# Decoder trunk on one core: hop steps get priority, columns end where outputs or state are due, the embedding moves to other buffers

## Chip, cores and metric

The kernel runs on one core of a Trainium2 chip. The metric is the device time of one execution in microseconds, as the median of several runs.

## What is computed

One decoder layer on 512 tokens of width 2048, all in float32. Cut to what matters:

```python
h = rms_norm(x, norm_g)
z = h @ w_in                      # r,k,v,decay and rate inputs | rwkv gate | pool input | pool gate
zs = zs + (token_shift(zs) - zs) * mu
# RWKV group, 16 heads of 64:  S_t = S_{t-1}(diag(w_t) - kk_t^T (a_t kk_t)) + v_t^T k_t,  y_t = S_t r_t
y_rwkv = (head_group_norm(y) + bonus) * silu(g_rwkv)
# pool group, 4 groups of 256: window means over 2, 4, 8, 16 tokens minus the token
y_pool = (d @ w_pool) * pool_scale * silu(g_pool)
x = x + concat(y_rwkv, y_pool) @ w_out
x = x + sigmoid(x @ w_pg + b_pg) * (p @ w_ple)
return rms_norm(x, final_g)
```

The large products are made of three float32r products each (high x high, high x low, low x high). A weight tile is loaded by SyncE as `raw`, ScalarE converts it to `whi` (L132), VectorE takes the rest as `wlo` (L133). Activations are split the same way (L137, L138: `hhi`/`hlo`, `yhi`/`ylo`).

## The kernel before

Names: PE is TensorE, DVE is VectorE, ACT is ScalarE, SP is SyncE.

After the input norm the program runs eight rounds, one for each pair of heads (128 channels). A round's tokens are eight chunks of 64. The recurrence of a round goes from chunk to chunk by **hops**: `py<-sbd` (the state's part of the outputs, L753), `zs` on VectorE (L755), `pu<-zs` (L760), two copies `uv` on ScalarE (L763), `ps<-uv` (L768), and the state's two halves `sbd` on VectorE (L772 in the first chunk, L774 in others), which the next chunk's py reads. Each of these waits for the one before, so TensorE needs other work between them. That is the **stream**: the columns of `w_in` for the next round (`z` jobs), for the pool channels (`b` jobs, `pool_unit`), and at the end the embedding `p @ w_ple` (`embed_unit`). A column of 128 channels takes 48 products of 128x512 (`zcols`: 4 weight chunks of 12 products each). `pump(n)` takes products from the stream until n are done, and keeps a debt where it took more. `HC = (8, 8, 8)` says how many are wanted after each of the three products of a hop, and since they come in threes, links of six or nine arise. Halfway through a round `between()` pumps `H3` and `H2` products around `scores(j + 1)`, the next round's scores.

TensorE's instructions are kept in the order of the program (`pin`). VectorE, ScalarE and the queues get theirs from a scheduler, by priority and by its own estimate of when an operation is ready; each engine then runs its list in that order, so an operation that waits holds all behind it.

The pool (`pp`, two buffers a tag) holds the pool units' tiles `u`, `sw`, `sgp`, and `dh`/`dl` (one buffer each), the split input of the pool's product `wp`. The embedding's input `p` is transposed and split in the last round's `between()` into `hl`, which lies in the pool `rw` of the recurrence. Each embedding unit (512 columns) makes four row tiles `pple`; ScalarE copies each to `ple` (tags `u` and `sw`) and stores it to DRAM (L446, 256 KB).

After the rounds, the 16 tiles of the mixed output `yd` are loaded (`yin`, three buffers) and split to `yhi`/`ylo`, which lie where `rw` was: the first four by SP, the others by ACT (L891). Then comes the output projection (`acc_o`), weights `raw_o`/`whi_o`/`wlo_o`, and the gate product (`acc_g`). In the last 512 columns of it each of the four row tiles is finished in turn: `gate` adds the bias (L1012), takes tanh (L1013), and so on; `root` makes the norm's factor; `scaled` applies it and stores (L1053 for the last 512 columns, L1057 and L1059 for others).

Of the kernel before, what the change touches and what calls it, by code (L numbers as in the profile page):

```python
# [34 lines left out]
def trunk_kernel(ctx: ExitStack, tc: tile.TileContext, x, p, norm_g, w_in, mu, w0, w_up, a0, a_up,  # L35
# [157 lines left out]
    for j in range(NJ):  # L193
        if j + 1 < NJ:
            jobs += [("z", nm, j + 1) for nm in "krv"]
        jobs += [("b", None, n_ + i) for i in range(nfill[j])]
        n_ += nfill[j]
        if j + 1 < NJ:
            jobs += [("z", "g", j + 1)]
# [5 lines left out]
    for kind, nm, j in jobs:  # L205
        if kind == "z":
            plan_cols({"r": O_R, "k": O_K, "v": O_V, "g": O_G}[nm] + j * P, f"{nm}{j}")
        elif kind == "e":
# [174 lines left out]
    zt, dhl = {}, {}  # L383

    def zcols(ps, nm):
        for c in range(KT // CK):
            wh, wl = chunk(nm, c)
            for k in range(CK):
                kk = c * CK + k
                mm3(ps, wh[:, k, :], wl[:, k, :], hhi[:, kk, :], hlo[:, kk, :], kk == 0, kk == KT - 1)  # L390
                yield 3

    def pool_unit(n):
# [27 lines left out]
        for k in range(2):  # L421
            mm3(pq, wh[:, k, :], wl[:, k, :], dh[:, k, :], dl[:, k, :], k == 0, k == 1)
            yield 3
        m = 2 * g + i
        nc.vector.scalar_tensor_tensor(sgp, pq, dp(73, m), sgp, ALU.mult, ALU.mult)
        nc.scalar.dma_start(out=yd[NJ + m], in_=sgp)

    phl = []


    def embed_unit(ec):
        ws = [chunk(f"e{ec}_{k}", 0) for k in range(2)]
        phi, plo = phl
        for tt in range(NT):
            ts_ = slice(tt * P, (tt + 1) * P)
            pq = (psA, psM)[tt % 2].tile([P, EC], F32, name=f"pple{ec}_{tt}", tag=("acc", "m")[tt % 2])
            for k in range(2):
                wh, wl = ws[k]
                mm(pq, phi[:, k, ts_], wh[:, 0, :], start=k == 0, stop=False)
                mm(pq, phi[:, k, ts_], wl[:, 0, :], start=False, stop=False)  # L440
                mm(pq, plo[:, k, ts_], wh[:, 0, :], start=False, stop=k == 1)
                if k == 0:
                    yield 3
            t_ = pp.tile([P, EC], F32, name=f"ple{ec}_{tt}", tag=("u", "sw")[tt % 2])
            nc.scalar.copy(t_, pq)
            nc.scalar.dma_start(out=pled[ts_, ec * EC:(ec + 1) * EC], in_=t_)  # L446
            yield 3

    def stream():
        for kind, nm, j in jobs:  # L450
            if kind == "b":
                yield from pool_unit(j)
                continue
            if kind == "e":
                yield from embed_unit(j)
                continue
# [12 lines left out]
    def pump(n):  # L469
        debt[0] += n  # L470
        while debt[0] > 0:
            c = next(big, None)
            if c is None:
                debt[0] = 0
                return
            debt[0] -= c

    def need(nm, j):
# [246 lines left out]
    def recur(j, work, between):  # L725
# [17 lines left out]
        for ch in range(NCH):  # L743
# [8 lines left out]
            if ch > 0:  # L752
                mm(py[:, sl], ar[:, q, 2 * par:2 * par + 2, :], cur, start=ch in (1, 4), stop=True,  # L753
                                 skip_group_check=True)
                lead[0] = nc.vector.tensor_tensor(zs[pb:pb + 64], py[pb:pb + 64, sl], mv[pb:pb + 64, q, :], ALU.add)  # L755
                step()
# [4 lines left out]
            for h in range(2):  # L761
                hc = slice(64 * h, 64 * h + 64)
                nc.scalar.copy(uv[pb:pb + 64, ch, hc], psu[hc, hc])  # L763
            step()
            pump(HC2)
            if ch < NCH - 1:
                pss = psS.tile([P, T], F32, name=f"ps{j}_{ch}", tag="s")
                mm(pss[:, 0:P], bkn[:, ch, :], uv[:, ch, :], start=True, stop=True)  # L768
                for h in range(2):
                    hc = slice(64 * h, 64 * h + 64)  # L770
                    if ch == 0:
                        lead[0] = nc.vector.tensor_scalar(nxt[hc, hc], pss[hc, hc], pcc[hc], None, ALU.mult)  # L772
                    else:
                        lead[0] = nc.vector.scalar_tensor_tensor(nxt[hc, hc], pss[hc, hc], pcc[hc], s0p[hc, :],  # L774
                                                                 ALU.mult, ALU.add)
                s0p = rw.tile([P, C], F32, name=f"s0p{j}_{ch}", tag="s0p", bufs=2)
# [58 lines left out]
    HC, HT, HX = (8, 8, 8), 130, 16  # L835
    HS, HN = 9, 3
    pending = []
    need("k", 0)
# [13 lines left out]
    for j in range(NJ):  # L852
        def between():
            pump(H3)
            if j + 1 < NJ:
                scores(j + 1)
                pump(H2)
            else:

                phl.extend((hl[:, 0], hl[:, 1]))  # L860
                for k in range(2):
                    pt = psM.tile([P, T], F32, name=f"ppt{k}", tag="m")
                    for tt in range(NT):
                        tr(pt[:, tt * P:(tt + 1) * P], pn[:, tt, k * P:(k + 1) * P], ident)
                    split(phl[0][:, k, :], phl[1][:, k, :], pt)

        if j + 1 == NJ:
            pn = rw.tile([P, NT, DPLE], F32, name="pn", tag="ar", bufs=2)
            for h in range(2):
                nc.scalar.dma_start(out=pn[:, 2 * h:2 * h + 2, :],  # L870
                                    in_=p[256 * h:256 * h + 256, :].rearrange("(t p) q -> p t q", p=P))
            hl = rw.tile([P, 2, 2, T], F32R, name="hl", tag="mt", bufs=2)
        if j + 1 < NJ:
# [107 lines left out]
    with tc.tile_pool(name="fp", bufs=2) as fp, tc.tile_pool(name="kp_", bufs=1) as kp_:  # L981
# [20 lines left out]
        def gate(acc, ec, tt, cs, part):  # L1002
# [7 lines left out]
            else:  # L1010
                gt = fp.tile([P, w_], F32, name=f"gt{ec}_{tt}_{part}", tag="gt")
            nc.vector.tensor_tensor(gt, acc, bB[:, lc], ALU.add)  # L1012
            th = nc.scalar.activation(gt, gt, AF.Tanh, scale=0.5)  # L1013
# [12 lines left out]
            if ec < LAST:  # L1026
                nc.vector.tensor_tensor(x3[tt][:, cs], gt, gB[:, lc], ALU.mult)
            return gt, th, lead_

# [55 lines left out]
        for tt in range(NT):  # L1085
# [3 lines left out]
            for h, a_ in enumerate(acc[tt]):  # L1089
# [4 lines left out]
                with tc.high_priority(offset=TP * tt):  # L1094
                    g_, th_, lead_ = gate(a_, ec, tt, slice(ec * EC + hc.start, ec * EC + hc.stop), ec + h)
                gts.append(g_)
                if tt == NT - 1 and h == 1:
                    rs_, gts_ = rest
# [33 lines left out]
```

## Time and profile before

| | |
|---|---|
| median of 3 runs | 1124.58 us (1123.9 to 1125.92) |
| profiled execution | 1124.75 us |
| its span | 1123.0 us |
| mean granted TensorE clock | 0.991 of full speed |
| TensorE busy | 1080.0 us, 96% |
| VectorE / ScalarE / GpSimd busy | 63% / 40% / 6% |

TensorE is busy throughout, with three thin places: the start (input norm), the passage from the embedding to the output projection at some 743 to 752 us, and the end. The time between is 8 rounds of some 75 us from about 130 to 720, and two large projections from 752 to 1112. The view of waits names who ended each idle time of an engine; the timeline gives start, duration, engine, line and tiles of each instruction, and in brackets the idle time before it with its releaser. Matmuls are pipelined: one of 128x512 is shown with 0.39 us, but the next starts sooner.

### The profile page before, as it was taken

To read this page: it belongs to the slowest core of one execution; us is meant where nothing else is said; L and a number is where in the kernel's file an instruction comes from. 1 tells how busy PE (TensorE), PEld (TensorE's weight loads), DVE (VectorE), ACT (ScalarE), POOL (GpSimd) and SP (SyncE) were. 2 spreads that over 40 slices of the span, in tenths; PEclk is the share of its full clock that TensorE was granted. 3 is DMA by queue.
4 is the path that set the end of the run, shared out by engine and by line. 5 is a ranking of instruction groups with operands and counts; after the bars stand their busy time and mean duration, and the time that the engine had idled before them with its cause. 6 is when DMAs were issued, how large, how long until landed. Compare 5 with 4: busy or idle time off the path is not lost. (4 is left out here: it accounts for less than half of the span.)

```text
span 1123.0 us, 17267 instructions
## 1 busy us (share of the span) xinstructions
PE 1080.0 (96%) x6090; PEld 881.8 (79%) x6090; DVE 707.6 (63%) x1835; ACT 450.1 (40%) x917; POOL 68.5 (6%) x180
## 2 busy tenths in 40 slices
PE   5999999999999999999999999969999999999996
PEld 4888887877877877878778777758888888888885
DVE  7677868788579688786885946524424323345265
ACT  7633435334335353353352433444222222233246
POOL 2100110110010000201101001000000000000000
PEclk9999999999999999999999999979999999999998
DMA  7433432433423333323234332478434437355444
GB/s 228 121 92 93 109 97 76 110 87 80 114 80 100 102 83 91 97 76 108 81 91 118 90 117 66 136 252 256 163 99 164 136 127 227 111 188 144 146 132 150
DMA packets 178485, 138.56 MB, mean 123 GB/s; under 512 B 34677, under 2 KB 139742, under 8 KB 178398
## 3 DMA queue, kind: packets, MB, share of 16 engines
q1 hardware_dynamic: 158270, 104.94, 31.8%
q10 hardware_dynamic: 20128, 32.52, 9.1%
q8 instruction: 48, 0.79, 0.3%
q14 instruction: 39, 0.32, 0.1%
HBM read 118.02 MB, written 18.87 MB: 122 GB/s over the span
## 5 line engine op out<-in xcount | busy, mean ns | idle before, releaser
L133 DVE TENSOR_TENSOR wlo_g<-raw_g,whi_g 128x512 fp32r<-128x512 f32 x88 | 59.4, 684 | 85.7 <-ACT whi_g L132 83.4
L156 PE MATMUL acc_o<-whi_o,yhi 128*128 128x512 f32 x256 | 100.5, 396 | 9.3 <-ACT whi_o L132 9.3
L156 PE MATMUL zb<-hhi,whi_b 128*128 128x512 f32 x256 | 108.2, 423 | 0.0
L133 DVE TENSOR_TENSOR wlo_o<-raw_o,whi_o 128x512 fp32r<-128x512 f32 x64 | 43.9, 691 | 94.5 <-ACT whi_o L132 94.5
L132 ACT CAST whi_g<-raw_g 128x512 fp32r<-128x512 f32 x88 | 54.4, 621 | 118.0 <-PE acc_g L156 74.3
L156 PE MATMUL acc_o<-whi_o,ylo 128*128 128x512 f32 x256 | 101.3, 396 | 0.0
L156 PE MATMUL acc_o<-wlo_o,yhi 128*128 128x512 f32 x256 | 101.2, 395 | 0.0
L156 PE MATMUL zb<-hhi,wlo_b 128*128 128x512 f32 x256 | 100.7, 393 | 0.0
L156 PE MATMUL zb<-hlo,whi_b 128*128 128x512 f32 x256 | 100.0, 391 | 0.0
L156 PE MATMUL acc_g<-whi_g,x2hi 128*128 128x512 f32 (+1 forms) x224 | 86.8, 388 | 0.0
L156 PE MATMUL acc_g<-wlo_g,x2hi 128*128 128x512 f32 (+1 forms) x224 | 86.5, 386 | 0.0
L156 PE MATMUL acc_g<-whi_g,x2lo 128*128 128x512 f32 x224 | 86.1, 386 | 0.0
L132 ACT CAST whi_o<-raw_o 128x512 fp32r<-128x512 f32 x64 | 39.8, 623 | 100.5 <-PE acc_o L156 96.2
L132 ACT CAST whi_b<-raw_b 128x512 fp32r<-128x512 f32 x64 | 39.7, 620 | 76.2 <-PE zv L156 34.5
L781 POOL TENSOR_SCALAR s0p<-sbd,pw 64x64 f32<-64x64 f32 x96 | 48.8, 508 | 342.0 <-DVE sbd L774 257.1
L133 DVE TENSOR_TENSOR wlo_b<-raw_b,whi_b 128x512 fp32r<-128x512 f32 x64 | 43.9, 687 | 35.4 <-ACT whi_b L132 32.7
L156 PEld LDWEIGHTS acc_o<-whi_o,yhi 128*128 128x128 f32 x256 | 48.8, 191 | 19.6 <-issue 9.7
L156 PEld LDWEIGHTS acc_o<-wlo_o,yhi 128*128 128x128 f32 x256 | 48.8, 190 | 10.7 <-DVE wlo_o L133 0.5
L156 PEld LDWEIGHTS zb<-hhi,wlo_b 128*128 128x128 f32 x256 | 48.1, 188 | 11.2
L156 PEld LDWEIGHTS acc_o<-whi_o,ylo 128*128 128x128 f32 x256 | 48.8, 191 | 9.9
L630 DVE TENSOR_TENSOR xw<-xw,tm 128x60 f32<-128x60 f32 (+24 forms) x248 | 52.0, 210 | 6.7
L156 PEld LDWEIGHTS zb<-hhi,whi_b 128*128 128x128 f32 x256 | 48.4, 189 | 8.5
(281 smaller groups left out, 2537.9 us busy)
## 6 DMA issues: line engine op xcount, KB each, us to landing
raw_b<-in_w_in_dram SPq DMA_DIRECT2D x64, 256.0 KB
raw_o<-in_w_out_dram SPq DMA_DIRECT2D x64, 256.0 KB
raw_g<-in_w_pg_dram SPq DMA_DIRECT2D x64, 256.0 KB
raw_k<-in_w_in_dram SPq DMA_DIRECT2D x32, 256.0 KB
raw_r<-in_w_in_dram SPq DMA_DIRECT2D x32, 256.0 KB
raw_v<-in_w_in_dram SPq DMA_DIRECT2D x32, 256.0 KB
raw_g<-in_w_in_dram SPq DMA_DIRECT2D x32, 256.0 KB
n<-nd SPq DMA_DIRECT2D x16, 256.0 KB
```

The lines of the kernel that those rows point to most:

```text
L132: nc.scalar.copy(hi, raw)
L133: nc.vector.tensor_tensor(lo, raw, hi.bitcast(F32), ALU.subtract)
L156: i = nc.tensor.matmul(*a, **k)
L630: nc.vector.tensor_tensor(xw[:, 0:n_, s + 1:32], xw[:, 0:n_, s + 1:32], tm[:, 0:n_, 0:w_], ALU.add)
L781: nc.gpsimd.tensor_scalar(s0p[hc, :], nxt[hc, hc], pcn[hc], None, ALU.mult)
```

## The change

1. `zs`, `uv` and `sbd` are issued with a priority raised by `HP = 1000`, for the scheduler's order on VectorE and ScalarE.
2. The stream keeps its place within a column (`place`). After `scores(j + 1)` the new `pump_to(H2)` takes that many products that the place comes nearest to a multiple of 24 or to 6 beyond it. The pool units' six `wp` products are no longer counted. The last round's `between()` pumps 8 instead of `H3`.
3. The transposes and splits of `p` become a job of the stream ahead of pool unit 14. Their results lie in the tags `u` and `sw`, the embedding's row tiles in `dh`/`dl`, two row tiles a buffer: 8 stores of 512 KB instead of 16 of 256 KB. `hl` is gone.
4. In the tail, the scaling of the last 512 columns of tile tt - 1 is issued after the sum of tile tt (for tt 1 and 2).

```diff
@@ jobs
-        jobs += [("b", None, n_ + i) for i in range(nfill[j])]
+        for i in range(nfill[j]):
+            jobs += [("p", None, 0)] if n_ + i == 14 else []
+            jobs += [("b", None, n_ + i)]
@@ zcols
                 mm3(ps, wh[:, k, :], wl[:, k, :], hhi[:, kk, :], hlo[:, kk, :], kk == 0, kk == KT - 1)
+                place[0] = 3 * (kk + 1)
                 yield 3
@@ pool_unit
             mm3(pq, wh[:, k, :], wl[:, k, :], dh[:, k, :], dl[:, k, :], k == 0, k == 1)
-            yield 3
+            yield 0
@@ embed_unit
-        phi, plo = phl
+        outs = [pp.tile([P, 2, EC], F32, name=f"ple{ec}_{i}", tag=("dh", "dl")[i], bufs=1) for i in range(2)]
...
-            t_ = pp.tile([P, EC], F32, name=f"ple{ec}_{tt}", tag=("u", "sw")[tt % 2])
-            nc.scalar.copy(t_, pq)
-            nc.scalar.dma_start(out=pled[ts_, ec * EC:(ec + 1) * EC], in_=t_)
+            t_ = outs[tt // 2]
+            nc.scalar.copy(t_[:, tt % 2, :], pq)
+            if tt % 2 == 1:
+                rows = slice((tt - 1) * P, (tt + 1) * P)
+                nc.scalar.dma_start(out=pled[rows, ec * EC:(ec + 1) * EC].rearrange("(t p) n -> p t n", p=P), in_=t_)
@@ stream
+            if kind == "p":
+                for k in range(2):
+                    pt = psM.tile([P, T], F32, name=f"ppt{k}", tag="m")
+                    for tt in range(NT):
+                        tr(pt[:, tt * P:(tt + 1) * P], pn[0][:, tt, k * P:(k + 1) * P], ident)
+                    a_ = pp.tile([P, T], F32R, name=f"phi{k}", tag="u")
+                    b_ = pp.tile([P, T], F32R, name=f"plo{k}", tag="sw")
+                    split(a_, b_, pt)
+                    phl.append((a_, b_))
+                yield 3
+                continue
@@ new, beside pump
+    def pump_to(n):
+        debt[0] += n
+        unit, half = sum(HC), HC[2] - 2
+        off = (place[0] + debt[0]) % unit
+        debt[0] += min((-off, half - off, unit - off), key=abs)
+        pump(0)
@@ recur (the same around uv and both forms of sbd)
-                lead[0] = nc.vector.tensor_tensor(zs[pb:pb + 64], py[pb:pb + 64, sl], mv[pb:pb + 64, q, :], ALU.add)
+                with tc.high_priority(offset=HP):
+                    lead[0] = nc.vector.tensor_tensor(zs[pb:pb + 64], py[pb:pb + 64, sl], mv[pb:pb + 64, q, :],
+                                                      ALU.add)
@@ between
-            pump(H3)
+            pump(H3 if j + 1 < NJ else HC[2])
             if j + 1 < NJ:
                 scores(j + 1)
-                pump(H2)
-            else:
...
+                pump_to(H2)
@@ tail
+                if 0 < tt < NT - 1:
+                    rs_, gts_ = rest
+                    with tc.high_priority(offset=TP * tt), tc.issue_after(sum_.ins):
+                        scaled(tt - 1, rs_, gts_, (LAST,))
...
-                    scaled(tt, rs, gts, (0, 2) if tt == NT - 2 else range(LAST + 1))
+                    scaled(tt, rs, gts, (0, 2) if tt == NT - 2 else range(LAST))
```

**TensorE, round 1, chunks 1 to 2**, from three products behind `ps1_1` on to the next py. Before (`zg2`, `zk3` are columns of rounds 2 and 3):

```order
L156 MATMUL zg2_2668<-hhi_134,whi_g2_3_1524 128x512
L156 MATMUL zg2_2668<-hlo_135,whi_g2_3_1524 128x512
L156 MATMUL zg2_2668<-hhi_134,wlo_g2_3_1525 128x512
L156 MATMUL zk3_2820<-hhi_134,whi_k3_0_1530 128x512
L156 MATMUL zk3_2820<-hlo_135,whi_k3_0_1530 128x512
L156 MATMUL zk3_2820<-hhi_134,wlo_k3_0_1531 128x512
L156 MATMUL py1_0_2620<-sbd0_566,ar1_1647 128x128
```

The changed kernel, from the same place:

```order
L156 MATMUL zg2_2668<-hhi_134,whi_g2_3_1524 128x512
L156 MATMUL zg2_2668<-hlo_135,whi_g2_3_1524 128x512
L156 MATMUL zg2_2668<-hhi_134,wlo_g2_3_1525 128x512
L156 MATMUL py1_0_2617<-sbd0_566,ar1_1647 128x128
L156 MATMUL zk3_2822<-hhi_134,whi_k3_0_1530 128x512
L156 MATMUL zk3_2822<-hlo_135,whi_k3_0_1530 128x512
L156 MATMUL zk3_2822<-hhi_134,wlo_k3_0_1531 128x512
```

With the three products ahead of these rows, py stood nine products behind ps before, and stands six behind it now, at the column's end.

**VectorE, round 2, chunk 5**: the state's halves `sbd0`, from `ps2_5`, beside a column's weights (`wlo_v4_3`) and work for round 3 (`tm3`, `xw3`, of the triangular inverse). Before:

```order
L626 TENSOR_TENSOR tm3_3876<-xw3_3875,n323_1_3693 128x6x11
L133 TENSOR_TENSOR wlo_v4_3_2194<-raw_v4_3_2191,whi_v4_3_2193 128x512
L630 TENSOR_TENSOR xw3_3875<-xw3_3875,tm3_3876 128x6x11
L361 SCALAR_TENSOR_TENSOR sr4_4063<-zr4_3893,prm_131,sr4_4063 128x511
L774 SCALAR_TENSOR_TENSOR sbd0_566<-ps2_5_4082,pw2_2389,s0p2_4_4003 64x64 x2
L626 TENSOR_TENSOR tm3_3876<-xw3_3875,n323_1_3693 128x6x10
```

The changed kernel (L807 is the line of `sbd`, L785 that of `zs`):

```order
L655 TENSOR_TENSOR tm3_3873<-xw3_3872,n323_1_3699 128x6x11
L807 SCALAR_TENSOR_TENSOR sbd0_566<-ps2_5_4063,pw2_2383,s0p2_4_3988 64x64
L133 TENSOR_TENSOR wlo_v4_3_2194<-raw_v4_3_2191,whi_v4_3_2193 128x512
L807 SCALAR_TENSOR_TENSOR sbd0_566<-ps2_5_4063,pw2_2383,s0p2_4_3988 64x64
L659 TENSOR_TENSOR xw3_3872<-xw3_3872,tm3_3873 128x6x11
L365 SCALAR_TENSOR_TENSOR sr4_4076<-zr4_3916,prm_131,sr4_4076 128x511
L785 TENSOR_TENSOR zs0_568<-py2_4_3935,mv2_3416 64x128
```

The state's halves moved ahead of `sr4` and `xw3`, and the weights' split now stands between them.

**ScalarE, the end of the embedding**: copies of unit 3 (`ple3_*`), conversions `yhi` of the loaded `yin`, and the projection's first weights `whi_o0_8`. Before:

```order
L137 CAST yhi_7927<-yin8_7929 128x512
L445 COPY ple3_3_8092<-pple3_3_8085 128x512
L137 CAST yhi_7927<-yin9_7933 128x512
L137 CAST yhi_7927<-yin10_7937 128x512
L446 DMA pled_137<-ple3_3_8092 128x512
L891 DMA yin12_8095<-yd_136 128x512
L891 DMA yin13_8099<-yd_136 128x512
L137 CAST yhi_7927<-yin11_7941 128x512
L132 CAST whi_o0_8_8152<-raw_o0_8_8150 128x512
```

The changed kernel, at the copies of unit 2:

```order
L137 CAST yhi_7962<-yin8_7964 128x512
L137 CAST yhi_7962<-yin9_7968 128x512
L137 CAST yhi_7962<-yin10_7972 128x512
L456 DMA pled_137<-ple1_1_7935 128x2x512
L453 COPY ple2_0_8010<-pple2_0_8012 128x512
L453 COPY ple2_0_8010<-pple2_1_8020 128x512
L137 CAST yhi_7962<-yin11_7976 128x512
```

And at the end of unit 3:

```order
L453 COPY ple3_1_8047<-pple3_2_8065 128x512
L453 COPY ple3_1_8047<-pple3_3_8073 128x512
L916 DMA yin13_8086<-yd_136 128x512
L456 DMA pled_137<-ple3_1_8047 128x2x512
L916 DMA yin0_8090<-yd_136 128x512
L137 CAST yhi_7962<-yin13_8086 128x512
L916 DMA yin1_8094<-yd_136 128x512
L132 CAST whi_o0_8_8139<-raw_o0_8_8137 128x512
```

The conversions of yin8 to yin10 moved from behind unit 3's third copy to ahead of unit 2's first; the projection's first weights stand behind one more load and conversion (yin13).

## Rows read from the trace of the kernel before

**Rows 1.** The page: busy time of each engine, share of the span, instructions.

```profile
PE 1080.0 (96%) x6090; PEld 881.8 (79%) x6090; DVE 707.6 (63%) x1835; ACT 450.1 (40%) x917; POOL 68.5 (6%) x180
```

**Rows 2.** Waits of TensorE: whom for, us in total, times, longest.

```profile
PE acc_o L156 <- ACT whi_o L132: 9.3, 1, 9.3
...
PE py L156 <- DVE sbd L774: 5.1, 8, 1.1
...
PE pu L156 <- DVE zs L755: 1.1, 3, 0.7
...
PE ps L156 <- ACT uv L763: 0.5, 1, 0.5
```

**Rows 3.** Timeline of all engines (start, us, engine, line), round 7, from 698.7.

```profile
698.70 0.38 PE L156 MATMUL ps<-uv,bkn 128*128 128x128 f32 x2
...
699.28 0.59 DVE L774 SCALAR_TENSOR_TENSOR sbd<-ps,pw,s0p 64x64 f32<-64x64 f32 x2
...
700.31 0.38 PE L156 MATMUL py<-sbd,ar 128*128 128x128 f32 x2
```

**Rows 4.** Timeline, round 7, one chunk later, from 704.9.

```profile
704.91 0.38 PE L156 MATMUL ps<-uv,bkn 128*128 128x128 f32 x2
...
705.61 0.69 DVE L365 SCALAR_TENSOR_TENSOR sgp<-sgp,zb 128x512 f32<-128x512 f32 x1
...
706.21 0.59 DVE L774 SCALAR_TENSOR_TENSOR sbd<-ps,pw,s0p 64x64 f32<-64x64 f32 x2
...
706.86 0.49 PE L156 MATMUL py<-sbd,ar 128*128 128x128 f32 x2 [0.17 <-DVE sbd L774]
```

**Rows 5.** Timeline, round 4, a link of nine products, from 455.1.

```profile
455.13 0.62 ACT L132 CAST whi_r<-raw_r 128x512 fp32r<-128x512 f32 x1 [1.43 <-PE zk L156]
455.16 0.38 PE L156 MATMUL ps<-uv,bkn 128*128 128x128 f32 x2
455.65 0.27 DVE L774 SCALAR_TENSOR_TENSOR sbd<-ps,pw,s0p 64x64 f32<-64x64 f32 x1 [2.13 <-PE ps L156]
...
455.85 0.67 DVE L133 TENSOR_TENSOR wlo_r<-raw_r,whi_r 128x512 fp32r<-128x512 f32 x1
...
456.56 0.29 DVE L774 SCALAR_TENSOR_TENSOR sbd<-ps,pw,s0p 64x64 f32<-64x64 f32 x1
```

**Rows 6.** Timeline of SP, ACT and PE, embedding to projection, 732 to 753.

```profile
732.41 1.03 SPq L129 DMA_DIRECT2D raw_o<-in_w_out_dram  x2
...
732.88 0.81 ACTq L446 DMA_DIRECT2D pled<-ple  x2
...
737.47 0.59 ACT L445 COPY ple<-pple 128x512 f32<-128x512 f32 x1 [2.66 <-DMA pled<-ple]
...
742.97 5.36 SPq L891 DMA_DIRECT2D yin<-yd  x4
...
746.64 0.62 ACT L137 CAST yhi<-yin 128x512 fp32r<-128x512 f32 x1 [3.78 <-DMA yin<-yd]
...
751.47 0.61 ACT L132 CAST whi_o<-raw_o 128x512 fp32r<-128x512 f32 x1
...
752.18 0.77 PE L156 MATMUL acc_o<-whi_o,yhi 128*128 128x512 f32 x1 [9.28 <-ACT whi_o L132]
```

**Rows 7.** Waits of SyncE's DMA queue, the one for the embedding.

```profile
SPq L891 <- PE pple L156: 9.5, 1, 9.5
```

**Rows 8.** 725 to 750 us: busy times, granted TensorE clock, DMA share, GB/s.

```profile
725.00:750.00 25.00, 17.90 (x77) 14.13 (x75) 4.94 (x8) 11.50 (x21) 0.00 (x0) 0.90 0.76 250
```

**Rows 9.** Timeline of DVE and PE in the tail.

```profile
1101.19 0.75 DVE L1053 SCALAR_TENSOR_TENSOR x<-gt,frs,gB 128x512 f32<-128x512 f32 x1
1101.86 0.68 DVE L1012 TENSOR_TENSOR gt<-acc_g,bB 128x512 f32<-128x512 f32 x1
...
1112.39 0.28 PE L156 MATMUL acc_h<-whk,x2lo 128*128 128x256 f32 x1
...
1112.92 0.41 DVE L1012 TENSOR_TENSOR gt<-acc_h,bB 128x256 f32<-128x256 f32 x1
```

More of the change, by code (lines that the diff above doesn't have):

```diff
@@ L207, in trunk_kernel @@
             plan_cols({"r": O_R, "k": O_K, "v": O_V, "g": O_G}[nm] + j * P, f"{nm}{j}")
+        elif kind == "p":
+            continue
         elif kind == "e":
@@ L383, in trunk_kernel @@
     zt, dhl = {}, {}
+    place = [0]
     def zcols(ps, nm):
@@ L426, in pool_unit @@
         nc.scalar.dma_start(out=yd[NJ + m], in_=sgp)
-    phl = []
+    phl, pn = [], []
     def embed_unit(ec):
         ws = [chunk(f"e{ec}_{k}", 0) for k in range(2)]
-        phi, plo = phl
+        outs = [pp.tile([P, 2, EC], F32, name=f"ple{ec}_{i}", tag=("dh", "dl")[i], bufs=1) for i in range(2)]
         for tt in range(NT):
@@ L438, in embed_unit @@
                 wh, wl = ws[k]
-                mm(pq, phi[:, k, ts_], wh[:, 0, :], start=k == 0, stop=False)
-                mm(pq, phi[:, k, ts_], wl[:, 0, :], start=False, stop=False)
-                mm(pq, plo[:, k, ts_], wh[:, 0, :], start=False, stop=k == 1)
+                phi, plo = phl[k]
+                mm(pq, phi[:, ts_], wh[:, 0, :], start=k == 0, stop=False)
+                mm(pq, phi[:, ts_], wl[:, 0, :], start=False, stop=False)
+                mm(pq, plo[:, ts_], wh[:, 0, :], start=False, stop=k == 1)
                 if k == 0:
                     yield 3
-            t_ = pp.tile([P, EC], F32, name=f"ple{ec}_{tt}", tag=("u", "sw")[tt % 2])
-            nc.scalar.copy(t_, pq)
-            nc.scalar.dma_start(out=pled[ts_, ec * EC:(ec + 1) * EC], in_=t_)
+            t_ = outs[tt // 2]
[3 more added lines that the diff above has]
+                nc.scalar.dma_start(out=pled[rows, ec * EC:(ec + 1) * EC].rearrange("(t p) n -> p t n", p=P), in_=t_)
             yield 3
@@ L455, in stream @@
                 yield from embed_unit(j)
+                continue
+            if kind == "p":
[8 more added lines that the diff above has]
+                yield 3
                 continue
@@ L762, in recur @@
                 hc = slice(64 * h, 64 * h + 64)
-                nc.scalar.copy(uv[pb:pb + 64, ch, hc], psu[hc, hc])
+                with tc.high_priority(offset=HP):
+                    nc.scalar.copy(uv[pb:pb + 64, ch, hc], psu[hc, hc])
             step()
@@ L770, in recur @@
                     hc = slice(64 * h, 64 * h + 64)
-                    if ch == 0:
-                        lead[0] = nc.vector.tensor_scalar(nxt[hc, hc], pss[hc, hc], pcc[hc], None, ALU.mult)
-                    else:
-                        lead[0] = nc.vector.scalar_tensor_tensor(nxt[hc, hc], pss[hc, hc], pcc[hc], s0p[hc, :],
-                                                                 ALU.mult, ALU.add)
+                    with tc.high_priority(offset=HP):
+                        if ch == 0:
+                            lead[0] = nc.vector.tensor_scalar(nxt[hc, hc], pss[hc, hc], pcc[hc], None, ALU.mult)
+                        else:
+                            lead[0] = nc.vector.scalar_tensor_tensor(nxt[hc, hc], pss[hc, hc], pcc[hc], s0p[hc, :],
+                                                                     ALU.mult, ALU.add)
                 s0p = rw.tile([P, C], F32, name=f"s0p{j}_{ch}", tag="s0p", bufs=2)
@@ L836, in trunk_kernel @@
     HS, HN = 9, 3
+    HP = 1000
     pending = []
@@ L853, in between @@
         def between():
-            pump(H3)
+            pump(H3 if j + 1 < NJ else HC[2])
             if j + 1 < NJ:
                 scores(j + 1)
-                pump(H2)
[L858 to L865, printed above, removed]
+                pump_to(H2)
         if j + 1 == NJ:
-            pn = rw.tile([P, NT, DPLE], F32, name="pn", tag="ar", bufs=2)
+            pn.append(rw.tile([P, NT, DPLE], F32, name="pn", tag="ar", bufs=2))
             for h in range(2):
-                nc.scalar.dma_start(out=pn[:, 2 * h:2 * h + 2, :],
+                nc.scalar.dma_start(out=pn[0][:, 2 * h:2 * h + 2, :],
                                     in_=p[256 * h:256 * h + 256, :].rearrange("(t p) q -> p t q", p=P))
-            hl = rw.tile([P, 2, 2, T], F32R, name="hl", tag="mt", bufs=2)
         if j + 1 < NJ:
@@ L1011, in gate @@
                 gt = fp.tile([P, w_], F32, name=f"gt{ec}_{tt}_{part}", tag="gt")
-            nc.vector.tensor_tensor(gt, acc, bB[:, lc], ALU.add)
+            sum_ = nc.vector.tensor_tensor(gt, acc, bB[:, lc], ALU.add)
             th = nc.scalar.activation(gt, gt, AF.Tanh, scale=0.5)
@@ L1027, in gate @@
                 nc.vector.tensor_tensor(x3[tt][:, cs], gt, gB[:, lc], ALU.mult)
-            return gt, th, lead_
+            return gt, sum_, th, lead_
         def root(tt, parts, meanwhile=None):
@@ L1094, in trunk_kernel @@
                 with tc.high_priority(offset=TP * tt):
-                    g_, th_, lead_ = gate(a_, ec, tt, slice(ec * EC + hc.start, ec * EC + hc.stop), ec + h)
+                    g_, sum_, th_, lead_ = gate(a_, ec, tt, slice(ec * EC + hc.start, ec * EC + hc.stop), ec + h)
                 gts.append(g_)
+                if 0 < tt < NT - 1:
+                    rs_, gts_ = rest
+                    with tc.high_priority(offset=TP * tt), tc.issue_after(sum_.ins):
+                        scaled(tt - 1, rs_, gts_, (LAST,))
                 if tt == NT - 1 and h == 1:
```

## The prediction

> **What bounds the kernel now.** The page comes first: TensorE is busy for 1080.0 us (96%) of the span of 1123.0, VectorE 63%, ScalarE 40% [rows 1]. So the whole kernel is one stream of products, and only the some 43 us in which TensorE stands still can be won or added to. The second view lists what TensorE waited for [rows 2]. One wait of 9.3 us stands at the first product of the output projection. Three entries belong to the hops of the recurrence: 5.1 us in 8 waits of py for the state (sbd), 1.1 in 3 of pu for zs, 0.5 in 1 of ps for uv, in all 6.7 us in 12 waits. The third view is the timeline at single hops. After ps there are products of the column stream as cover, then py. With six of them and VectorE free, py starts 1.61 us after ps (698.70, 700.31), while the state is ready at 699.28 + 0.59 = 699.87, some 0.4 us early [rows 3]. In the other example VectorE was in a 0.69 us operation at 705.61, the state's first half came only at 706.21, and py at 706.86, so 1.95 us after ps: 0.34 us lost where the wait shows 0.17 [rows 4]. So a wait costs about 0.17 more than it shows, and the hops' price now is 6.7 + 12 x 0.17 = **8.7 us**. This is what priority and phase can win, at most.
>
> **The change, priority and phase.** The two must be read together. Priority puts zs, uv and sbd ahead of other ready work; no work is added. The phase decides how many products cover each link. By TensorE's order, before, the link from ps to py has nine products in rounds 0, 1, 3, 4 and 6, and six in rounds 2, 5 and 7 (15 links, without the one in each round at which the outputs of half a round stand). Now it has six in rounds 0 to 6, 35 links, and round 7 has nine; uv and y have nine there instead. So the longest chain of a cycle has the least cover. With VectorE free it still fits, by the 0.4 us of [rows 3], and uv and zs, which fitted with six in some rounds, get more. That is the good side: a queue of one operation no longer stalls them.
>
> The other side is in VectorE's order (round 2 above): in rounds 2, 4 and 6 a wlo split (L133) stands between the two halves of sbd in 14 of the six-product links. The split waits for ScalarE's conversion of the same weights, which waits for the last product that reads the old ones. The trace has just this in round 4, there with nine products: ps at 455.16, conversion 455.13 for 0.62, first half at 455.65, split 455.85 for 0.67, second half 456.56 + 0.29 = 456.85 [rows 5]. That is 1.69 us after ps, and py follows a state by some 0.05 (706.21 + 0.59 = 706.80, py at 706.86, [rows 4]), so 1.74. Behind nine products no py waited for that; behind six it is due at 1.61 [rows 3]. Each such link then loses 1.74 - 1.61 = 0.13 us, 14 of them **1.8 us**. Bounds: 0 where the split is quicker, 0.75 each (10.5 us) where ScalarE comes to the conversion one operation of 0.62 us late.
>
> What else stays of the stalls? The order still has other operations ahead of a hop, and runs as written, not by who is ready first. Counting the work on VectorE between a hop's product and its operation at the durations of its rows, places with over 0.5 us go from 21 to 14, and the longest are shorter. I leave 2.5 of the 8.7 us (bounds 0.5 and 5). Hops after: 1.8 + 2.5 = 4.3, so the term is 4.3 - 8.7 = **-4.4 us** (-7 to 0 without late conversions).
>
> The other, smaller waits of TensorE between 75 and 745 us are off these chains; what is held behind a hop's operation on VectorE waits at most its 0.3 us (0.27 and 0.29, [rows 5]), and weights are split a chunk of twelve products ahead. I take 0, bounds -1 and +1. The wp products are the same, no longer counted, so they are six products of extra cover where they stand; the eight transposes of p are the same work earlier: 0. TensorE has as many instructions as before.
>
> **The transition to the output projection.** Before, the projection's first product comes at 752.18 after 9.28 us without work [rows 6]. SyncE's loads of y could go only when the last products of the embedding had read hl, a wait of 9.5 us [rows 7]; they go at 742.97, the first lands for its conversion at 746.64, and whi_o is made from 751.47 to 752.08 [rows 6]. Now hl is gone, and loads can go during the embedding. What is late next? ScalarE runs in order, and in its new order (above) the conversions of yin8 to 10 stand ahead of unit 2's copies, the load of yin13 behind the last copies, and whi_o behind yhi13. Copies empty PSUM, so the embedding itself now waits for those loads. The walk, with all up to here as before: the loads follow the third of raw_o, before at 732.41, so go at some 732.8, land 3.6 later as before (742.97 to 746.64), and three conversions of 0.62 bring unit 2's first copy to 738.3. Copies come in pairs of some 1.2 (two of 0.59, [rows 6]), and each pair writes a buffer that the store of two pairs earlier must have left. A store issued at 732.88 held its buffer until 737.47, 4.6 us [rows 6]; I take that for twice the bytes too, since half as many are in flight. The store of pair 3 goes at 738.3, so pair 5 is copied from 742.9 to 744.1; the store of that holds until 748.7, and pair 7 is copied to 749.9. Then yin13 lands at 753.5, and two conversions end at 754.7 instead of 752.1: +2.6. With stores as quick as the loads, 3.6, the same walk ends at 752.7: +0.6. With stores of 6 for twice the bytes it is +5.4, and -4 if the loads hold no copy up (the embedding then ends as before, 9.3 before 752.18, and its last copy, load and two conversions take some 5). Between +0.6 and +2.6 I take **+1.5 us**. Either way TensorE idles for 5 us or more, so the granted clock falls here as before, 0.90 in 725 to 750 [rows 8], and gives nothing back.
>
> A row speaks against a large gain here: the DMA engines' share is 0.76 at 250 GB/s in 725 to 750 [rows 8], so loads put earlier share them with the stores. The Trainium skill (DMA: Bandwidth & Descriptors, section "Issuing engines are not separate DMA queues") says that transfers started by SyncE and ScalarE run on the same 16 engines and interleave, and that a second issuer saves only the issue time. By that rule alone the transition would come out near 0 rather than at -4, since the same bytes move before whi_o is due; the share of 0.76 agrees in part.
>
> **The tail.** The scaling L1053 of 0.75, issued at 1101.19, is right ahead of the next tile's sum at 1101.86 [rows 9]. Behind the sum it lies in the time in which VectorE waits for ScalarE's tanh. But TensorE's last product comes at 1112.39 and ends 0.28 later, and the last sum came at 1112.92 [rows 9]: some 0.25 us is there, and a little in ScalarE's queue behind it. **-0.3 us** (0 to -0.6).
>
> **Sum.** 1124.75 is the profiled execution's time (span 1123.0), and the median of the three runs is 1124.58, so the same. 1124.75 - 4.4 + 1.5 - 0.3 = 1121.55, **1121.5 us**.
>
> **Rivals.**
> - Transition pays: loads land beside the embedding without holding its copies. For it: the wait for hl was the one named releaser. Against: the order on ScalarE, the DMA share. -4.4 - 4 - 0.3 gives 1116.0.
> - Priority does little: the order on VectorE was already near what it can be, and the hops keep 6.7 of 8.7 us because twenty more links are short. For it: the stall of [rows 4] is in a six-product link, and twenty more links get six. -2 + 1.5 - 0.3 gives 1124.0, no change.
> - Slower: late conversions in the short links. If ScalarE is in another operation of some 0.62 us when the old weights come free, the split and with it the second half come 0.62 later: 14 x 0.75 = 10.5 us, hops 13.0 instead of 8.7, the sum 1124.75 + 4.3 + 1.5 - 0.3 = 1130.2. It decides from 0.53 us a link (14 x 0.53 + 2.5 - 8.7 + 1.2 = 2.2). Against it: in round 4 the conversion stood at 0.03 before ps and was never late there.
>
> **How the numbers follow.** Forecast 0.45, transition pays 0.20, little 0.22, slower 0.13. About 0.2% (2.2 us) is what a measurement of this kernel can tell from no change, so faster means under 1122.3 and slower over 1126.8. The forecast's own spread (hops, transition) is some 3 us to both sides: of its 0.45, 0.31 lies below 1122.3, 0.13 between, 0.01 above. With the rivals: faster 0.31 + 0.20 + 0.05 = 0.56, same 0.13 + 0.15 + 0.02 = 0.30, slower 0.14. The range reaches down to the first rival, 1115.5, and up past the second, 1126.0; its own range for the likeliest is 1118.5 to 1124.5.
>
> **What would show it.** The waits of py for sbd: about 14 of some 0.1 us, all in rounds 2, 4, 6, and hardly any of 1 us; pu and ps near none. A link with a split between: py 1.74 us after ps. The first acc_o product not before that of before, counted from the embedding's start, the pple products now waiting for ScalarE's copies, an idle time before acc_o of 5 to 9. In the tail the scaling behind the sum. Wrong it would be if py waits 0.5 us or more in the links with a split, if the embedding is not held up, or if stalls of zs and uv persist.

## The result

The changed kernel is slower: 1131.08 us (1130.0 to 1133.18, 5 runs) against 1125.02 (1123.9 to 1126.07, 5 runs), ratio 1.0050 with a 95% interval of 1.0039 to 1.0062. The forecast was 1121.5, range 1115.5 to 1126.0.

The profiled execution is the slowest of the five, 1133.18 us, with a span of 1131.5, so 8.4 us stand between the two traces, 6.1 between the medians. Its busy times, which answer to [rows 1]:

```profile
PE 1086.9 (96%) x6090; PEld 882.2 (78%) x6090; DVE 707.5 (63%) x1835; ACT 449.1 (40%) x917; POOL 76.9 (7%) x180
```

TensorE's idle time is 44.6 us (1131.5 - 1086.9), against 43.0 before. So only 1.6 of the 8.5 us between the spans are idle time. For the other 6.9 the same 6090 products were shown as busy longer: some ran at a lower clock (below), and some stalls are too short to be shown as waits. Waits of TensorE after (us in total, times, longest), which answer to [rows 2]:

```profile
PE pple L156 <- ACT ple L453: 6.1, 2, 5.5
PE py L156 <- DVE sbd L807: 5.0, 13, 0.7
PE acc_o L156 <- issue: 4.3, 1, 4.3
...
PE pyt L160 <- DVE ysb L852: 1.8, 3, 0.7
PE pm L156 <- DVE bk L603: 1.6, 2, 1.5
PE acc_o L156 <- DVE wlo_o L133: 0.8, 3, 0.3
PE pbk L160 <- ACT sig L530: 0.8, 2, 0.4
...
PE ps L156 <- ACT uv L795: 0.2, 1, 0.2
```

One line of the same view before, for comparison:

```profile
PE pyt L160 <- DVE ysb L819: 0.3, 1, 0.3
```

The 8 waits of py, up to 1.1 us long, became 13 shorter ones with nearly the same total. Two entries are new, pple for ScalarE's copies and pbk. The waits of pyt (the transposes of the previous round's outputs, behind the group norm) grew from 0.3 to 1.8 us.

TensorE's starts put against those of before, place by place, give where the time came up. At the first chunk of round 0 the changed kernel is 0.2 us behind, at the first product of the embedding 3.3 (723.25 against 719.90), at the first product of the projection 7.1 (759.26 against 752.18), at its last product 8.5 (943.67 against 935.19), and at VectorE's last scaling 8.5 as well (1126.36 against 1117.82). So the rounds cost 3.1, the passage from embedding to projection 5.1 (3.7 of it up to the projection's first product, the rest within its first 80 products), and the tail gave nothing.

**A link with the split between.** Timeline of the changed kernel at 295 us (start, us, engine, line), which answers to [rows 5]:

```profile
295.37 0.38 PE L156 MATMUL ps<-uv,bkn 128*128 128x128 f32 x2
295.38 0.62 ACT L132 CAST whi_k<-raw_k 128x512 fp32r<-128x512 f32 x1 [1.47 <-issue]
...
295.86 0.28 DVE L807 SCALAR_TENSOR_TENSOR sbd<-ps,pw,s0p 64x64 f32<-64x64 f32 x1 [2.11 <-PE ps L156]
...
296.06 0.68 DVE L133 TENSOR_TENSOR wlo_k<-raw_k,whi_k 128x512 fp32r<-128x512 f32 x1
...
296.76 0.29 DVE L807 SCALAR_TENSOR_TENSOR sbd<-ps,pw,s0p 64x64 f32<-64x64 f32 x1
...
297.11 0.38 PE L156 MATMUL py<-sbd,ar 128*128 128x128 f32 x1
```

py comes 1.74 us after ps, as worked out, and loses 0.13.

**A link late in a round.** The same view at 251 us, where ps starts at 251.34 and the inverse of the next round (tm, xw) is on VectorE:

```profile
251.49 0.69 DVE L133 TENSOR_TENSOR wlo_b<-raw_b,whi_b 128x512 fp32r<-128x512 f32 x1
252.10 0.18 DVE L659 TENSOR_TENSOR xw<-xw,tm 128x28 f32<-128x28 f32 x1
...
252.75 0.18 DVE L655 TENSOR_TENSOR tm<-xw,n 128x16 f32<-128x16 f32 x1
252.85 0.59 DVE L807 SCALAR_TENSOR_TENSOR sbd<-ps,pw,s0p 64x64 f32<-64x64 f32 x2
...
253.49 0.38 PE L156 MATMUL py<-sbd,ar 128*128 128x128 f32 x1 [0.38 <-DVE sbd L807]
```

ps could be read some 0.5 us after its start, at 251.83 (295.37 to 295.86 above). But VectorE was in the weights' split until 252.18, had four small operations of the inverse behind that, and came to the state at 252.85. py is 2.15 us after ps, 0.54 late. The likely reason is that the list was ordered by an estimate of when ps is ready, and that VectorE had fallen behind that estimate; the rows show only the order and the lateness.

**pyt.** Timeline at 346 us, and the granted clock (the column ahead of the DMA share) behind it; before, pyt at 347.73 waited for nothing and the clock in 349 to 353 was 1.00:

```profile
346.97 0.69 PE L160 MATMUL pyt<-ident,ysb 128*128 128x128 f32 x2 [0.41 <-DVE ysb L852]
348.38 0.77 PE L160 MATMUL pyt<-ident,ysb 128*128 128x128 f32 x2 [0.72 <-DVE ysb L852]
```

```profile
349.00:353.00 4.00, 4.00 (x12) 3.14 (x12) 3.58 (x2) 0.78 (x1) 0.00 (x0) 0.57 0.22 66
```

After these waits TensorE starts products 0.43 us apart for a while instead of 0.23, at the level of 1.2 GHz, and 1.6 us are lost. Six profiles have these two waits. Three have the dip behind them (0.57 here, 0.57 without the embedding's buffers, 0.61 with the late loads), and three have a granted clock of 1.00 there (the phase alone, the norm's priority, the early finish). So the dip falls in some executions only.

**The passage.** Timeline of SyncE, ScalarE and TensorE, 736 to 760 us, which answers to [rows 6]; the embedding starts at 723.25:

```profile
736.83 1.86 SPq L916 DMA_DIRECT2D yin<-yd  x3
...
743.23 0.62 ACT L137 CAST yhi<-yin 128x512 fp32r<-128x512 f32 x1 [5.94 <-DMA yin<-yd]
...
744.60 0.32 SPq L916 DMA_DIRECT2D yin<-yd  x1
...
745.93 1.07 ACT L453 COPY ple<-pple 128x512 f32<-128x512 f32 x2
746.57 0.80 PE L156 MATMUL pple<-whi_e,phi 128*128 128x512 f32 x1 [5.55 <-ACT ple L453]
...
747.28 0.62 ACT L137 CAST yhi<-yin 128x512 fp32r<-128x512 f32 x1 [0.27 <-DMA yin<-yd]
...
759.26 0.77 PE L156 MATMUL acc_o<-whi_o,yhi 128*128 128x512 f32 x1 [4.33 <-issue]
```

Three loads went 13.6 us after the embedding's start, and the first took 6.4 us to its conversion. In that time ScalarE stood for 5.94 us with the copies of unit 2 behind it. The load issued at 744.60 had little beside it (the next store was issued at 745.46), and was there for the conversion at 747.28, 2.7 us later. The idle time of 9.28 became two, 5.55 and 4.33, each with a dip of the clock. The first dip lies within the embedding (granted clock 0.50), and unit 3's copies then wait for TensorE:

```profile
748.00:752.00 4.00, 4.00 (x11) 3.11 (x10) 0.62 (x1) 1.66 (x3) 0.00 (x0) 0.50 0.80 298
```

```profile
752.10 0.59 ACT L453 COPY ple<-pple 128x512 f32<-128x512 f32 x1 [1.21 <-PE pple L156]
```

From 746.57 to 752.26 there are 13 products in 5.7 us; at 0.23 us apart they would take 3.0, so this dip costs 2.7. The waits themselves (6.1 for the copies and 4.3 ahead of the projection) are 1.1 over the 9.3 of before. Together that is 3.8 us, against the 3.7 found up to the projection's first product.

### The profile page after: what moved, and what is told of

It reads as the page before. It is cut to its first block, busy times and chain, and to the rows that moved or that the text cites. A ratio compares the mean times of both kernels' runs of the same rounds, so it can differ in the third digit from the quotient of the medians.

```text
span 1131.5 us, 17256 instructions
## 1 busy us (share of the span) xinstructions
PE 1086.9 (96%) x6090; PEld 882.2 (78%) x6090; DVE 707.5 (63%) x1835; ACT 449.1 (40%) x917; POOL 76.9 (7%) x180
## 4 chain that ended last, share of the span: by engine, by line
PE 51%; DVE 5%; DMA 3%; ACT 2%; issue 1%; ACTq 0%; SPq 0%; DVEq 0%
PE acc_o L156 14%; PE acc_g L156 14%; PE zb L156 9%; PE zg L156 3%; DMA yin<-yd 2%; PE zk L156 2%; PE zr L156 2%; PE pple L156 1%; PE py L156 1%; DVE tm L655 1%; DVE xw L659 1%; DVE wlo_b L133 1%; PE pp L156 1%; PE px L996 1%; PE pu L156 1%
## 5 line engine op out<-in xcount | busy, mean ns | idle before, releaser
L814 POOL TENSOR_SCALAR s0p<-sbd,pw 64x64 f32<-64x64 f32 x96 | 55.8, 581 | 330.9 <-DVE sbd L807 269.5
L156 PEld LDWEIGHTS zb<-hhi,wlo_b 128*128 128x128 f32 x256 | 48.3, 189 | 11.3
```

Source lines behind the costliest of these rows:

```text
L156: i = nc.tensor.matmul(*a, **k)
L814: nc.gpsimd.tensor_scalar(s0p[hc, :], nxt[hc, hc], pcn[hc], None, ALU.mult)
```

## The experiments

Ratios are to the kernel before in the same set of runs, with their 95% intervals. Its median went from 1125.0 to 1126.1 us between sets, so times of different sets can be compared to about 1 us.

**The parts alone.** Priority alone (the three `high_priority` blocks and `HP`):

> The kernel before with the priority of zs, uv and sbd alone. Theory A (the six-product state links and the order that comes with them lose the time in the rounds; priority by itself is good): the hop waits of TensorE fall from 6.7 us in 12 waits to under 3, the transposes of the outputs (pyt) wait as before (0.3 us), and the time is 3 to 5 us under before, some 1121. Theory B (priority holds up the rest of VectorE, the group norm ahead of pyt among it): waits of pyt of 1.5 us and more as in the changed kernel, and the time is at or over before, 1125 to 1128.

Measured: 1121.91 us, 0.9968 (0.9955 to 0.9980). Waits of TensorE:

```profile
PE py L156 <- DVE sbd L778: 2.0, 6, 0.5
...
PE ps L156 <- ACT uv L766: 0.8, 1, 0.8
```

Theory A holds: the hop waits fall to 3.2 us (with 0.4 for pu), and pyt's stay at 0.3. In the profile the embedding starts at 715.60, 4.3 us before that of the kernel before.

The phase alone (`place`, `pump_to`, `yield 0`):

> The kernel before with the columns' phase alone (place, pump_to, the uncounted wp products), without priority. Theory A: the state links of six products have all of VectorE's queue ahead of them, hop waits rise over 6.7 us, to 10 or more, and some 14 links lose 0.13 us without a wait; the time is 4 to 8 us over before, 1129 to 1133, more than the 3.2 us that the changed kernel loses in the rounds. Theory B: hop waits stay about 7 us, pyt waits 0.3 us, the time is within 2 us of before.

Measured: 1130.24, 1.0038 (1.0024 to 1.0051).

```profile
PE py L156 <- DVE sbd L784: 6.3, 13, 1.0
...
PE pyt L160 <- DVE ysb L829: 1.8, 3, 0.7
```

The phase brings the waits of pyt by itself, without priority. The hop waits stay at 6.8 us (with 0.5 for ps) and do not rise to 10, so that part of theory A missed; its time is right, and theory B is out. In the profile the embedding starts 3.3 us late (723.22), as in the changed kernel, and 2.6 us more are lost behind it.

The shown waits leave out stalls without a wait, so the links themselves were measured in the same way in every trace: from start to start, over the 1.61 us of an undisturbed link of six products or the 2.30 of nine (0.23 more for each further product). Summed over all hops, that is 12.3 us before, 11.6 in the changed kernel, 6.8 with priority alone and 14.8 with the phase alone. Priority wins 5.4 us at the hops, and the phase takes most of it back.

The embedding's buffers alone:

> The kernel before with the embedding's new buffers alone (transposes of p as a job, two row tiles a store, 8 in place of the last round's 16 products between). Both theories of the rounds: no change up to the embedding but in the last round. If the early loads of y hold up the embedding as in the changed kernel (one wait of 5.5 us for ScalarE's copy, then 4.3 ahead of the projection): 4 to 6 us over before, 1129 to 1131. If that hold-up came only with the changed order of the rounds ahead of it: within 1 us of before or under it.

Measured: 1123.79, 0.9986 (0.9977 to 0.9995), so a small gain. Its loads of y go 5.4 us after the embedding's start, the embedding waits 3.4 us, and 4.3 are left ahead of the projection, in all 1.6 less than the 9.3 of before; ahead of the embedding, the last round is 2.7 us shorter. The second expectation holds. A hold-up is there, but smaller: the loads went ahead of most of the stores.

All but the embedding:

> The changed kernel without the embedding's new buffers: priority, phase and tail. If the parts add up: the rounds lose 3 us as in the changed kernel, the transition is as before (9.3 us of idle time), so 1127 to 1128.5. If the embedding's job in the stream is what disturbs the rounds: 1120 to 1123.

Measured: 1128.33, 1.0024 (1.0014 to 1.0034). The rounds lose 3.8 us to the embedding's start, much as with the embedding changed, and the first expectation holds. But priority and phase do not add up: in the profiles priority alone gained 4.3 there and the phase alone lost 3.3, and the two together lose 3.8, of which 1.6 are the dip that the phase's own profile did not have. The embedding gains 1.6 alone and costs 2.7 on top of these.

**The state link.** One line in `pump_to`:

```diff
         debt[0] += min((-off, half - off, unit - off), key=abs)
         pump(0)
+        debt[0] -= 2
```

> The kernel without the embedding's buffers (priority, phase, tail; 1128.3) with one line more in pump_to: two products of debt are kept, so that the link from py to pu gets six products and those to ps and to the next py nine, in rounds 0 to 6. If the short state link is what costs (7.5 us of waits and 1.9 without a wait): the waits of py for sbd fall under 3 us, no link with a split between loses 0.13, and the time is 6 to 8 us lower, 1120.5 to 1122.5. If the hops' waits only move to pu for zs (now six products): 1126 to 1128. The waits of pyt (4.5 us, and 1.4 at the lower clock) should stay in both.

Measured: 1128.90, 1.0022 (1.0013 to 1.0031), which neither expectation had. No py waits any more, and the links of all hops fall from 11.6 us over their cover to 5.4, but the time is the same, and the embedding starts where it did (723.80, against 723.68 without this line):

```profile
PE pyt L160 <- DVE ysb L834: 3.9, 1, 3.9
PE pm L156 <- DVE bk L585: 3.6, 3, 2.2
...
PE pu L156 <- DVE zs L767: 2.2, 6, 0.6
PE pss L156 <- ACT bkn L680: 1.8, 3, 0.7
```

What the hops gave is waited for between the rounds. The next round's preparation is a chain on VectorE and ScalarE, and a TensorE that leaves the hops sooner stands there instead. A sum over hop waits is thus not a gain by itself.

**The wait of pyt.** First, the raised priority for the eight operations of the group norm ahead of it:

> The changed kernel with the raised priority for the group norm's last eight operations (ysb, ahead of pyt) as well. If pyt waits because VectorE's order puts other work of the next round ahead of them: waits of pyt under 0.5 us, no lower clock behind them at 350 us, 5 us less, 1126. If they come as early as their inputs allow: pyt waits as before, 1131.

Measured: 1131.38, 1.0047 (1.0034 to 1.0061), pyt as before (1.8 us in 3). VectorE's order around the norm is the same as without it, and the eight operations start at 346.34 in both. Their inputs come from a chain of small operations with one of the preparation between most of them. That chain was not raised, so what an earlier norm would bring was not tried. Then more cover:

```diff
-    H1, H2, H3, H4, H5, HE = 6, 16, 16, 8, 10, 32
+    H1, H2, H3, H4, H5, HE = 6, 16, 16, 8, 18, 32
-    HC, HT, HX = (8, 8, 8), 130, 16
+    HC, HT, HX = (8, 8, 8), 130, 8
```

> The changed kernel with the previous round's finish (the transposes pyt) eight products later in a round's preparation: 18 products ahead of it instead of 10 and 8 behind it instead of 16. If pyt waits because TensorE comes to it sooner than in the kernel before while the group norm's chain takes as long (the waits on bkn ahead of it are gone): pyt waits under 0.5 us in all (1.8 in 3 waits, 4.5 with what lies around them), no lower clock behind it, 4 to 5 us less, 1126 to 1127. If the group norm comes later as well: 1130 to 1131.

Measured: 1124.59, 0.9996 (0.9987 to 1.0005), 6.5 us under the changed kernel. No wait of pyt is left in the profile, and no dip. The embedding starts at 716.75, 3.2 us before that of the kernel before, so with more cover the rounds are faster than before and not slower. The cause of the rounds' loss is thus cover against the norm's end. The expectation's reason for the lack of cover does not hold in round 3, where TensorE comes to pyt no sooner than before: there the norm's last eight operations start 10.0 us behind the last product of outputs (336.31 to 346.34) instead of 8.4 (337.63 to 345.99), since three operations of the preparation moved ahead of them. In rounds 1, 2, 4 and 5 there are three products fewer between the two places (24 instead of 27). Which of the two weighs more was not separated. The later finish was not run on the kernel before, so it is open how much of the 6.5 us mends the loss and how much any of these kernels would gain.

**The passage.** Loads sooner, by 16 instead of 32 products ahead of the last finish (`HE = 16`):

> The changed kernel with 16 in place of 32 products between the last round and its finish (HE). The store of the last round's outputs, which the first load of y waits for because it is put where they lie, then goes 3.7 us sooner against the embedding's start. If that wait is what makes the loads late and collide with the stores: first load some 6 to 8 us after the embedding's start and not 13.6, the wait of 5.5 us of the embedding for ScalarE's copies falls to some 3 or less, 3 to 5 us less, 1126 to 1128. If the hold-up comes from the order of ScalarE alone (copies behind the conversions of y): 1130 to 1132.

Measured: 1130.81, 1.0045 (1.0031 to 1.0059), no gain. The loads went at 8.8 us after the embedding's start, and still:

```profile
736.52 0.62 ACT L137 CAST yhi<-yin 128x512 fp32r<-128x512 f32 x1 [6.55 <-DMA yin<-yd]
```

They met the stores of unit 0 and weight loads there, and the first took 6.2 us. Sooner is not enough; ScalarE stands in order at a load in flight either way. So the conversions were put behind the copies, by writing the loads behind the embedding:

```diff
-    for k in order[:4]:
-        load_y(k, nc.sync)
     pump(10 ** 6)
+    for k in order[:4]:
+        load_y(k, nc.sync)
```

> The changed kernel with the first four loads of y and their splits written behind the embedding instead of ahead of it, so that they come behind its copies in ScalarE's order, one conversion between two pairs of copies. If the hold-up is ScalarE's, standing in order at conversions of loads that are still in flight with copies behind it: TensorE's waits in the embedding fall from 6.1 us to under 1, the projection starts 30 to 32 us after the embedding's start (36.0 in the changed kernel), 4 to 5 us less, 1126 to 1127. If the stores and loads in flight together are the limit, the wait only moves behind the embedding: 1130 to 1131.

Measured: 1125.30, 0.9998 (0.9989 to 1.0007), 5.8 under the changed kernel. The projection starts 31.8 us after the embedding's start (722.47, 754.29) instead of 36.0. But the embedding still waits 3.5 us, not under 1; ScalarE now waits for a store:

```profile
742.58 1.08 ACT L453 COPY ple<-pple 128x512 f32<-128x512 f32 x2 [6.05 <-DMA pled<-ple]
743.54 0.63 ACT L137 CAST yhi<-yin 128x512 fp32r<-128x512 f32 x1
...
753.58 0.62 ACT L132 CAST whi_o<-raw_o 128x512 fp32r<-128x512 f32 x1 [1.85 <-issue]
```

So both theories have a share. The queue behind the load was one cost, and the conversions now lie between the copies, in part in the waits for stores; the collision of loads and stores is another, and stays. This profile has the dip behind pyt (0.61), so the gain is not from there.

**Together.** Without the phase, and without and with the late loads:

> The changed kernel without the columns' phase: priority, embedding and tail. If the parts add up (priority alone -3.6, embedding alone -1.6, tail near 0): -5, some 1120. If the embedding's new buffers cost what they cost in the changed kernel (5 us more for the stretch from its start to the projection): 1125. The first load of y then goes some 5 us after the embedding's start, as with the embedding alone, and not 13.6 as in the changed kernel.

Measured: 1123.19, 0.9977 (0.9968 to 0.9987). The first load goes 5.6 us after the embedding's start, as expected. The parts do not add: priority and embedding are no faster together than priority alone.

> Priority, embedding and tail without the phase (0.9977 of before), with the first loads of y behind the embedding. If ScalarE's order is what holds up: the embedding's wait of 3.6 us goes, 2 to 3 us less, 0.995 of before and the fastest of all. If loads and stores in flight are the limit: 0.9975, as without.

Measured: 1116.01 (1115.31 to 1116.88), 0.9924 (0.9910 to 0.9937), faster than both kernels and every other run, and 7.2 us under the run without the late loads, where 2 to 3 were expected. The embedding's wait for copies is 0.7 us, and 4.4 stay ahead of the projection:

```profile
PE acc_o L156 <- issue: 4.4, 1, 4.4
...
PE pple L156 <- ACT ple L450: 0.7, 1, 0.7
```

In this version the loads go 5.4 us after the embedding's start (721.47), each conversion of the four stands behind a copy (the first at 725.95), and none waits for its load. The transition is what the first rival had hoped for: the projection starts 27.3 us after the embedding (716.05, 743.39) instead of 32.3.

Three repairs of the changed kernel, with the long state link among them, and the two without it:

> The changed kernel with three repairs: two products of debt kept in pump_to (nine products in the state link), the finish eight products later, the loads of y behind the embedding. If each cause stands by itself: hops 10 to 4.4, pyt 4.5 to 0.5, transition 4 less: 1131 - 6 - 4 - 4 = 1117, under all others. If what is won in the hops comes back at the next waits (pm for bk and pss for bkn took 4 us of 6 in the run with the long state link): 1120 to 1123.

Measured: 1122.92, 0.9979 (0.9970 to 0.9988), the second expectation: pyt waits 2.5 us again, pss 2.0, pu 2.0.

> The changed kernel with the finish eight products later and the first loads of y behind the embedding, the state links short as in the changed kernel. If the transposes' wait and the hold-up of the embedding are two separate causes and the hops are as in the changed kernel: the gains add (1131.1 to 1124.6 and to 1125.3), 1118 to 1119.5. If they are one, or the one repair brings the loads back among the stores: 1122 to 1124.

Measured: 1119.79, 0.9947 (0.9933 to 0.9960). From 1131.1 that is 11.3 of the 12.3 that the two brought one by one, so they are two causes and make up the loss and more. The hops still cost what they cost in the changed kernel (py 4.5 us in 12 waits; 11.3 us of links over their cover).

## Why the prediction was wrong, point by point

- **What bounds.** The prediction let only the 43 us of idle time change. Idle time grew by 1.6 us and TensorE's busy time by 6.9, with the same 6090 products: the lower clock behind the waits and stalls that no wait shows. The hops' price of 8.7, the shown waits plus 0.17 each, was 12.3 when all links are measured. It was also read as a purse to be emptied; the run with the long state link shows that it is in part time that the preparation between rounds needs anyway.
- **Priority and phase, -4.4.** The sum was wrong because two edits with opposite signs were given one term. Priority alone measured -3.5 and phase alone +4.9 in their runs (from 1125.38). The links with a split cost 0.13 us each where VectorE was on time (seven of the 14, py 1.74 or 1.75 us after ps), but on average 0.32: 4.4 us instead of 1.8, since late in a round VectorE was behind as well. The residual of 2.5 was the second mis-sized term: the 21 other six-product links lost 4.2, most of it in the last two links of a round. State links lost 8.7 us, those of ps 0.4 and those of pu 2.5, in all 11.6 against 12.3 before: the term measured some -0.7 instead of -4.4. The count of operations ahead (21 places to 14) looked at the order, which cannot show that VectorE runs behind it. The sign that was named, about 14 short waits of py, came true by luck: the seven links that lose 0.13 show no wait, and the 13 waits stand late in rounds, seven of them in links without a split. One link with a split waited 0.6 us (331.06), which had been named as a sign of being wrong.
- **The other waits, 0 (bounds of 1).** The step that failed most in the rounds, and had hardly any working. Outside the hops the rounds lost 3.8 us: 3.5 from the product ahead of the transposes pyt to the one behind them, the dip 1.6, pbk 0.8, less 2.1 at pmv, pss and pp. With the hops' -0.7 that is the 3.1 of the rounds. A moved stream takes cover from one place of a round and gives it to another, and every one should have been checked against its chain.
- **The transition, +1.5 (to +5.4).** Right in mechanism and sign: loads during the embedding, copies of unit 2 held behind conversions, whi_o behind yin13. Measured +5.1, near the end of its bounds. The first mis-sized term is the landing of 3.6 us, taken from a place with three other loads: 6.4 here. The second is the clock, which was said to fall as before: it fell twice, and the dip within the embedding alone cost 2.7 us, and the last copies then waited for TensorE (1.21, 0.40 and 0.77 us), where the walk had them wait for stores. Some 1.4 us came up within the projection, in part at its waits for weights (0.8 and 0.3), for which there was no term. The Trainium skill's rule (DMA: Bandwidth & Descriptors, "Issuing engines are not separate DMA queues") spoke against a gain from early loads, and here the trace agrees: 6.4 us among other transfers, 2.7 with little beside it. The Trainium skill's fit for one transfer (DMA: Bandwidth & Descriptors, "Anatomy of one DMA", 2.0 us plus bytes at 436 GB/s, given for transfers that GpSimd issues) would make 2.6 for 256 KB, an estimate that only the second meets.
- **The tail, -0.3.** The scaling moved behind the sum, but the last sum came 0.96 us after TensorE's last product started (1120.88, 1121.84) instead of 0.53, and the end gained nothing. It was not run alone.
- **The rivals.** The slower one gave 1130.2, near the time, and was the wrong mechanism: in all 14 links with a split the conversion started within 0.04 us of ps (295.37, 295.38 above) and was not late. That the time came near its sum is luck. Its chance of 0.13 was too low because the phase's cost was looked for in one place only. The second rival had the hops nearly right, as they kept most of their price with more links short, but it had no loss between the rounds and a smaller one at the transition.

## What to carry to other kernels

When cover is moved among links of a chain, each place that gives cover up has to be set against its own chain, those between the rounds too; a wait taken away at one is often due at the next. A change that bundles an order and a distribution of work should be priced and tried as two. And an engine that runs in order should not be given an operation that waits for a transfer while others that free buffers stand behind it: here, putting four such operations behind that work gave 5.8 us in one version and 7.2 in another.

## What the runs showed of the hardware

The first of three loads of 256 KB, sent among stores and other loads, took 6.4 us to its conversion where one with little beside it took 2.7. Sent 4.8 us sooner, among other stores, the first still took 6.2 (730.35, 736.52), and nothing was gained. Waits of about 0.4 and 0.72 us ahead of two pairs of transposes (346.97 and 348.38 in the changed kernel) were followed by a stretch at a granted clock of 0.57 to 0.61 over 4 us in three profiles, and by 1.00 in three others.
